# Delta-rule copies with a scale, and the causal mask, on other engines, under a planner that puts two engines' reads of one PSUM tile in sequence

## The chip, the cores and the metric

The kernel runs on one core of a Trainium2 chip. A core has five engines with instruction streams of their own: TensorE (PE in the profile; its weight loads are listed as PEld), VectorE (DVE), ScalarE (ACT), GpSimd (POOL) and SyncE (SP), which here issues the DMAs. TensorE writes its results to PSUM, in eight banks; DVE and ACT read them there. The engines wait for one another through semaphores.

The metric is the device time of one execution in microseconds. The time before is the median of three runs.

## The reference

One inference step of a decoder trunk of two layers, in float32, for 512 prompt tokens and 8 x 8 sample tokens that share all weights; the model width is 1024. Layer 0 mixes by pooling, layer 1 by a gated delta rule; each mixer is followed by a SwiGLU feed-forward block (width 2816), and all of it sits between RMS norms. The change lies in the gated delta rule. In the reference it is, for each of 16 value heads, chunk by chunk:

```python
decay = jnp.exp(jnp.where(causal, gc[..., :, None] - gc[..., None, :], -jnp.inf))
kb = k * beta[..., None]
a_mat = jnp.where(strict, jnp.einsum('bhnid,bhnjd->bhnij', kb, k) * decay, 0.0)
...
qk = jnp.einsum('bhnid,bhnjd->bhnij', q, k) * decay
q_dec = q * jnp.exp(gc)[..., None]
k_dec = k * jnp.exp(gc[..., -1:] - gc)[..., None]
...
v_new = u_i - jnp.einsum('bhck,bhkv->bhcv', w_i, S)
o_i = jnp.einsum('bhck,bhkv->bhcv', qd_i, S) + jnp.einsum('bhcs,bhsv->bhcv', qk_i, v_new)
S = S * gl_i[..., None, None] + jnp.einsum('bhck,bhcv->bhkv', kd_i, v_new)
```

Here u and w are solutions of a unit lower triangular system with a_mat; q and k are normalised, with 8 heads of their own, each shared by two value heads.

## The kernel before

**How the order comes about.** The kernel's functions don't issue instructions; they record them in a list (Plan.put, line 334). At the end Plan.finish (line 400) simulates the core with a table of costs (Plan.cost, line 283), chooses the order in which each engine's instructions are issued (Plan.forward, line 537; an instruction recorded as EITHER goes to DVE or POOL as the plan decides), and emits them. That is why nearly all rows of the profile name line 447, where they are emitted. A long list of numbers (CHOSEN, line 79) stirs the ranks of the instructions in one stretch of planned time after another: each number gives one shift, written down beforehand, and the shifts are applied in turn (Plan.refined and Plan.moved, lines 449 and 468). Where the plan foresees a wait of TensorE it fills it with matmuls of ones (tile ps_w). Any change of a cost, of an operation or of a number in the list therefore changes the order of everything behind it, DMAs included.

In its simulation an instruction waits for its operands, for its engine and, on TensorE, for the free bank. Two engines that read one PSUM tile are free to overlap in it. The cost of issuing a DMA on SP is 400 or 350 ns by size (2500 between two DRAM tensors).

**Tiling.** Channels lie on the 128 partitions and tokens along the free axis. Prompt tokens are cut into four spans of 128; the 64 sample tokens ride along as a fifth. The big products use float32r matmuls in three passes (a high and a low part of weights and activations): each block of weights is loaded as wraw, ACT copies its high part into wh, and DVE or POOL subtracts to get wl (Weights.split). The small products of the delta rule are plain float32 matmuls.

**The delta-rule stage.** The 16 value heads are done in four groups G of four. project(G) (line 1425) makes q, k and v of a group: projection, a convolution of width four along time (tiles u and ac, three multiply-adds on DVE for each chunk), Silu, and transposes. Its finish (line 1463) gets the norms of q and k; there nk, rq, bet and gcq are scaled for the group. v of the prompt (vt) and of the samples (vs) is scaled out of PSUM by nk. core(G) (line 1789) then does the rule itself: QD gets the differences of the cumulated gates gc, loaded from DRAM (gc_d) by one DMA for each span, has the mask bar added (0 on and above the diagonal, -1e30 below it) and goes through Exp; products of q and k give Uw (the triangular matrices) and QD. inv32 (line 1318) inverts blocks of 32 by some sixty DVE operations (tiles ia and ii), braided with sample_front (line 1586); small matmuls build the whole inverse; then scan (line 1720) and sample_heads (line 1650) run side by side.

In scan, for each span s and each head pair hd: pk is the product of the state S with k and q; rs (DVE) subtracts the scaled first part from vt; t1 (DVE) is the second part scaled by gcq; pv is the inverse times rs; vn is pv scaled by bet (DVE), and ve is vn scaled by kde (EITHER); S grows by kt times ve; po is QD times vn, and vt gets po scaled by rq, plus t1. In the first span there is no state, so t1 and rs are left out and vt is po scaled by rq alone (DVE). The next span's pk waits for S, so ve lies on the chain from span to span, and t1 doesn't.

sample_heads does one step of the same kind for the 64 sample rows against eight loaded states (St), with rs on the lower and t1 on the upper 64 partitions of one pk bank; ve is split there into a high part vH (ACT) and a low part vL (EITHER) for float32r matmuls.

While core(G) waits on its chains, the plan has the projections of group G + 1, the gate's projections (zz) and the output of group G - 1 (zgate) to fill in. zgate scales vt, transposes it on TensorE and multiplies it by z, which is loaded from DRAM (vt from z_d).

Of the kernel before, what the change touches and what calls it, by code (L numbers as in the profile page):

```python
# [11 lines left out]
F32 = mybir.dt.float32  # L12
F32R = mybir.dt.float32r
I32 = mybir.dt.int32
AF = mybir.ActivationFunctionType
ALU = mybir.AluOpType
PSUM = bass.MemoryType.PSUM
DRAM = bass.MemoryType.DRAM
SB = bass.MemoryType.SB

P = 128
# [5 lines left out]
SMP = NB * NT  # L27
# [29 lines left out]
class Plan:  # L57
# [2064 lines left out]
```

## Time and profile before

| what | us |
|---|---|
| median of three runs | 1546.24 |
| lowest and highest of them | 1545.52 to 1547.1 |
| the profiled execution's own time | 1548.15 |
| its span, first to last instruction | 1546.4 |

The chain that ended last names PE for 85% of the span, DVE for 10%, DMAs for 2%. By stages the span is, roughly: pooling mixer up to 100 us, feed-forward of layer 0 up to 470, the delta rule up to about 1065, its output and the feed-forward of layer 1 to the end. The table of costs is the planner's own; every duration in this document is from the profile.

How to read what follows: a busy time is the union of an engine's instructions, so matmuls that overlap in the pipeline count once, and a wait that is shorter than the tail of the matmul before doesn't show as idle time. In groups of instructions, the columns are line, engine, operation, output <- inputs, shapes (partitions x elements), count, then the busy time in us, the mean ns of one, and the idle time ahead of them with what ended it. In tables by stretch of time, each row gives the stretch, its length and the busy us (and count) of PE, PEld, DVE, ACT and POOL, then the granted clock of TensorE, the DMA engines' share and GB/s.

### The profile page before, as it was taken

The page shows a single profiled execution, that of the slowest core. Times are in us where ns is not written, and L with a number is a line of the kernel's source. Part 1 is how long each engine was busy: PE and PEld are TensorE (multiplying, and loading weights), DVE is VectorE, ACT ScalarE, POOL GpSimd, SP SyncE. Part 2 cuts the span into 40 slices and gives each one's busy share as a digit, 9 for nine tenths or more (in the row PEclk, how much of TensorE's full clock was granted, in tenths as well). Part 3 has the DMA queues.
Part 4 walks back from the last instruction along what each step waited for, and adds up shares of the span by engine and source line. Part 5 has one row for each costly group of instructions (what it writes and reads, how often), then busy time and mean ns, then how long its engine had stood idle before and what let it go on. Part 6 is the DMA issues. An engine that isn't in the chain of part 4 may idle for free.

```text
span 1546.4 us, 30413 instructions
## 1 busy us (share of the span) xinstructions
PE 1522.8 (98%) x11899; PEld 1466.0 (95%) x11899; DVE 1181.3 (76%) x2360; ACT 791.1 (51%) x1655; POOL 130.4 (8%) x274
## 2 busy tenths in 40 slices
PE   8999999999999999999999999999999999999997
PEld 8999999999999998899899799899999999999997
DVE  5993566667787798997999799677896476757855
ACT  7753443435555965553553563525564543434553
POOL 4110000000000010221221210100110000000000
PEclk9999999999999999999999999999999999999999
DMA  6464333233466523345243343656855432323263
GB/s 187 127 194 116 90 87 92 88 89 109 135 177 173 147 82 109 93 122 141 72 139 106 108 141 113 198 156 208 246 172 159 120 94 85 99 79 110 77 172 107
DMA packets 344902, 197.86 MB, mean 128 GB/s; under 512 B 13547, under 2 KB 337740, under 8 KB 344751
## 3 DMA queue, kind: packets, MB, share of 16 engines
q1 hardware_dynamic: 344759, 195.92, 44.0%
q8 instruction: 94, 1.54, 0.4%
q14 instruction: 49, 0.40, 0.1%
HBM read 165.60 MB, written 30.52 MB: 127 GB/s over the span
## 4 chain that ended last, share of the span: by engine, by line
PE 85%; DVE 10%; DMA 2%; issue 1%; ACT 1%; POOL 0%; DVEq 0%; SPq 0%; ACTq 0%; POOLq 0%
PE ps_B L447 28%; PE ps_A L447 26%; PE ps_m L447 17%; PE ps_s L447 5%; PE ps_k L447 4%; PE ps_x L447 2%; PE ps_n L447 1%; PE ps_e L447 1%; DVE wl L447 1%; DVE Uw L447 1%; DVE ii L447 1%; DVE ac L447 1%; DMA vt<-z_d 1%; PE ps_g L447 1%; DMA QD<-gc_d 0%
## 5 line engine op out<-in xcount | busy, mean ns | idle before, releaser
L447 ACT ACTIVATE wh<-wraw 128x1024 fp32r<-128x1024 f32 (+4 forms) x240 | 233.4, 976 | 223.1 <-PE ps_A L447 79.5
L447 DVE TENSOR_TENSOR wl<-wraw,wh 128x1024 fp32r<-128x1024 f32 (+4 forms) x232 | 257.9, 1117 | 78.2 <-ACT wh L447 49.8
L447 PE MATMUL ps_m<-hH,wh 128*128 128x320 f32 (+1 forms) x832 | 249.5, 312 | 0.5 <-ACT u L447 0.3
L447 PE MATMUL ps_m<-hL,wh 128*128 128x320 f32 (+1 forms) x832 | 245.1, 306 | 0.3 <-DVE hL L447 0.3
L447 PE MATMUL ps_m<-hH,wl 128*128 128x320 f32 (+1 forms) x832 | 241.2, 305 | 0.0
L447 PEld LDWEIGHTS ps_m<-hH,wh 128*128 128x128 f32 x832 | 154.3, 189 | 5.6 <-issue 1.1
L447 PEld LDWEIGHTS ps_m<-hL,wh 128*128 128x128 f32 x832 | 154.5, 189 | 3.0 <-issue 0.6
L447 PEld LDWEIGHTS ps_m<-hH,wl 128*128 128x128 f32 x832 | 153.3, 189 | 2.0 <-issue 0.8
L447 PE MATMUL ps_B<-hH,wh 128*128 128x320 f32 (+1 forms) x444 | 128.3, 305 | 0.1
L447 PE MATMUL ps_B<-hH,wl 128*128 128x320 f32 (+1 forms) x444 | 127.9, 304 | 0.0
L447 PE MATMUL ps_B<-hL,wh 128*128 128x320 f32 (+1 forms) x444 | 127.5, 303 | 0.0
L447 PE MATMUL ps_A<-hL,wh 128*128 128x256 f32 (+1 forms) x432 | 120.4, 291 | 0.0
L447 PE MATMUL ps_A<-hH,wh 128*128 128x256 f32 (+1 forms) x432 | 119.7, 292 | 0.0
L447 PE MATMUL ps_A<-hH,wl 128*128 128x256 f32 (+1 forms) x432 | 119.1, 290 | 0.0
L447 PE MATMUL ps_B<-aH,wh 128*128 128x288 f32 x352 | 99.7, 298 | 0.2 <-DVE xa L447 0.2
L447 PE MATMUL ps_A<-aH,wl 128*128 128x288 f32 x352 | 99.3, 295 | 0.0
L447 PE MATMUL ps_A<-aH,wh 128*128 128x288 f32 x352 | 98.8, 297 | 0.2 <-DVE y L447 0.2
L447 PE MATMUL ps_B<-aL,wh 128*128 128x288 f32 x352 | 98.5, 297 | 0.0
L447 PE MATMUL ps_A<-aL,wh 128*128 128x288 f32 x352 | 97.9, 295 | 0.0
L447 PE MATMUL ps_B<-aH,wl 128*128 128x288 f32 x352 | 97.8, 296 | 0.0
L447 PEld LDWEIGHTS ps_B<-hH,wh 128*128 128x128 f32 x444 | 81.5, 188 | 1.3 <-ACT wh L447 0.5
L447 PEld LDWEIGHTS ps_B<-hH,wl 128*128 128x128 f32 x444 | 81.8, 188 | 0.1
(468 smaller groups left out, 4045.4 us busy)
## 6 DMA issues: line engine op xcount, KB each, us to landing
wraw<-in_ffn_w_in_dram SPq DMA_DIRECT2D x77, 512.0 KB
wraw<-in_gdn_w_in_dram SPq DMA_DIRECT2D x56, 512.0 KB
graw<-in_ffn_w_in_dram SPq DMA_DIRECT2D x33, 512.0 KB
wraw<-in_ffn_w_out_dram SPq DMA_DIRECT2D x32, 448.0 KB
wraw<-in_gdn_w_out_dram SPq DMA_DIRECT2D x24, 512.0 KB
wraw<-in_ffn_w_out_dram SPq DMA_DIRECT2D x32, 320.0 KB
St<-in_state_gdn_rec_dram SPq DMA_DIRECT2D x32, 256.0 KB
out_dram<-St SPq DMA_DIRECT2D x32, 256.0 KB
```

Of the source, the lines that this page charges most:

```text
L447: calls[e](*a, **k)
```

## The change

The planner:
- Plan.forward keeps, for each PSUM tile, when each engine's last read or write of it ends. An instruction on PE, ACT, DVE or POOL that touches a PSUM tile which another engine touched before is planned to end no earlier than if it had started behind that engine's end.
- An issue on SP is planned at 520 or 480 ns above 16384 elements (520 where the tile has two dimensions) and 460 or 360 below.
- The list of numbers is another one (four strings instead of five).

The operations:
- bk, a new small tile, is bet times kde, made once for each head pair (8 products of 128 x 10 in all).
- scan: t1 goes from one DVE product of 256 columns to two ACT copies of 128 columns with a scale for each partition; ve goes from EITHER, out of vn, to two ACT copies straight out of pv, with scale bk; vt of the first span goes from DVE to one ACT copy.
- sample_heads: t1 likewise; ve is no longer stored: vH is two ACT copies of pv scaled by bk, and vL two DVE operations, pv times bk minus vH.
- project: vs goes from DVE to ACT.
- core: the mask is no longer a tile that is added but an affine_select on POOL. The tile bar is gone.

```diff
@@ Plan.cost
-            hold = 2500.0 if out.space == DRAM and ins[0].space == DRAM else 400.0 if m > 16384 else 350.0
+            flat = len(list(out.ap)) == 2
+            hold = 2500.0 if out.space == DRAM and ins[0].space == DRAM else \
+                (520.0 if flat else 480.0) if m > 16384 else 460.0 if flat else 360.0
@@ Plan.forward
-            elif e in past:
-                if past[e][1] or ops[i][11]:
-                    late = max(past[e][0] + self.REBASE - t, 0.0)
-                    hold, done = hold + late, done + late
-                past[e] = t + done, ops[i][11]
+            elif e != "SP":
+                late = 0.0
+                for name in ops[i][10]:
+                    for other, end in read.get(name, {}).items():
+                        if other != e:
+                            late = max(late, end + self.LAT[e] - t)
+                if e in past and (past[e][1] or ops[i][11]):
+                    late = max(late, past[e][0] + self.REBASE - t)
+                hold, done = hold + late, done + late
+                if e in past:
+                    past[e] = t + done, ops[i][11]
+                for name in ops[i][10]:
+                    read[name] = {**read.get(name, {}), e: t + done}
@@ masks
-        bar = cst.tile([P, P], F32, name="bar")
-        DVE.tensor_scalar(bar, t_gt, -1e30, None, op0=mult)
@@ project, finish
+                            DVE.tensor_tensor(bk[:, :, h2], bet[:, :, h2], kde[:, :, h2], op=mult)
...
-                    DVE.tensor_scalar(vs[:SMP, i], pv, nk[:SMP, SPANS, kh:kh + 1], None, op0=mult)
+                    ACT.activation(vs[:SMP, i], pv, AF.Copy, scale=nk[:SMP, SPANS, kh:kh + 1])
@@ sample_heads
-                DVE.tensor_tensor(t1, pk[up, 0].rearrange("p (e v) -> p e v", e=2),
-                                  gcq[up, SPANS, h2].unsqueeze(2).to_broadcast([SMP, 2, P]), op=mult)
+                for e in range(2):
+                    ACT.activation(t1[:, e], pk[up, 0, e * P:(e + 1) * P], AF.Copy,
+                                   scale=gcq[up, SPANS, 2 * kh + e:2 * kh + e + 1])
...
-                EITHER.tensor_tensor(ve, vn, kde[:, SPANS, h2].unsqueeze(2).to_broadcast([P, 2, P]), op=mult)
...
-                split2(ve, vH, vL)
+                for e in range(2):
+                    by = bk[:, SPANS, 2 * kh + e:2 * kh + e + 1]
+                    ve = pv[:, 0, e * P:(e + 1) * P]
+                    ACT.activation(vH[:, e], ve, AF.Copy, scale=by)
+                    DVE.scalar_tensor_tensor(out=vL[:, e], in0=ve, scalar=by, in1=vH[:, e].bitcast(F32),
+                                             op0=mult, op1=sub)
@@ scan
-                        DVE.tensor_tensor(t1, pk[:, 1].rearrange("p (e v) -> p e v", e=2),
-                                          gcq[:, s, hh].unsqueeze(2).to_broadcast([P, 2, P]), op=mult)
+                        for e in range(2):
+                            ACT.activation(t1[:, e], pk[:, 1, e * P:(e + 1) * P], AF.Copy,
+                                           scale=gcq[:, s, hh.start + e:hh.start + e + 1])
...
-                    EITHER.tensor_tensor(ve, vn, kde[:, s, hh].unsqueeze(2).to_broadcast([P, 2, P]), op=mult)
+                    for e in range(2):
+                        ACT.activation(ve[:, e], pv[:, 0, e * P:(e + 1) * P], AF.Copy,
+                                       scale=bk[:, s, hh.start + e:hh.start + e + 1])
...
-                        DVE.tensor_scalar(vv, pov, rqc, None, op0=mult)
+                        ACT.activation(vv, pov, AF.Copy, scale=rqc)
@@ core
-                EITHER.tensor_tensor(de, de, bar.unsqueeze(1).to_broadcast([P, 4, P]), op=add)
+                POOL.affine_select(de, de, [[0, 4], [1, P]], ALU.is_ge, -1e30, base=0, channel_multiplier=-1)
```

More of the change, by code (lines that the diff above doesn't have):

```diff
@@ L557, in forward @@
             past = {"DVE": (0.0, False), "ACT": (0.0, False)}
+            read = {}
         else:
             todo, left, taken, free, ready, avail, when, mode, dma, port, phases, fast, recent, busy, turn, still, \
-                quiet, past = state
+                quiet, past, read = state
             left, taken, when, recent = left[:], taken[:], when[:], recent.copy()
-            free, mode, port, turn, still, quiet, past = (dict(v) for v in (free, mode, port, turn, still, quiet, past))
+            free, mode, port, turn, still, quiet, past, read = (
+                dict(v) for v in (free, mode, port, turn, still, quiet, past, read))
             ready = {e: v[:] for e, v in ready.items()}
@@ L704, in forward @@
         return (todo, left, taken, free, ready, avail, when, mode, dma, port, phases, fast, recent, busy, turn, still,
-                quiet, past, order, times)
+                quiet, past, read, order, times)
     def take(self, e, q, taken, mode):
@@ L798, in hybrid_kernel @@
     kde = sp.tile([P, SP1, VH], F32, name="kde")
+    bk = sp.tile([P, SP1, VH], F32, name="bk")
     gls = sp.tile([P, NB, VH], F32, name="gls")
@@ L859, in masks @@
         DVE.scalar_tensor_tensor(out=eye2, in0=eyo, scalar=par, in1=eye2, op0=mult, op1=add)
-        return t_gt, bar, s_le2, s_gt2, s_gt_r, s_in, s_st, eye2
+        return t_gt, s_le2, s_gt2, s_gt_r, s_in, s_st, eye2
     def dup(ap):
@@ L1308, in finish0 @@
                 pre_norm(tp, back[0], acc2, hf, G_MPRE + NC)
-            t_gt, bar, s_le2, s_gt2, s_gt_r, s_in, s_st, eye2 = masks(tp)
+            t_gt, s_le2, s_gt2, s_gt_r, s_in, s_st, eye2 = masks(tp)
             s_le = s_le2[:, :SMP]
@@ L1677, in sample_heads @@
                 sn = cp_.tile([P, 4, 2, P], F32, name="sn", tag="sn", bufs=1)
-                rs, t1, vn, ve = sn[lo, 0], sn[up, 1], sn[:, 2], sn[:, 3]
+                rs, t1, vn = sn[lo, 0], sn[up, 1], sn[:, 2]
                 for e in range(2):
```

225 rows, old and new, of the table CHOSEN are left out of this document.

## The prediction

> **What bounds the kernel now.** I read the page first: busy time by engine and the slices.
>
> ```profile
> PE 1522.8 (98%) x11899; PEld 1466.0 (95%) x11899; DVE 1181.3 (76%) x2360; ACT 791.1 (51%) x1655; POOL 130.4 (8%) x274
> ...
> DVE  5993566667787798997999799677896476757855
> ```
>
> TensorE (PE) is the bound of the whole: 1522.8 of 1546.4 us. The change takes no matmul away, so it can only win time in which PE stands still. VectorE (DVE) is at 76% in the mean, but its slices show mostly nines from the fifteenth to the twenty-fifth (541 to 966 us); that is the delta-rule core. So I split the span by stage.
>
> ```profile
> core 0: us, PE busy (x) PEld busy (x) DVE busy (x) ACT busy (x) POOL busy (x), PEclk, DMA share, GB/s
> 0.00:40.00 40.00, 35.43 (x230) 32.13 (x230) 24.02 (x67) 29.35 (x70) 16.39 (x75) 0.91 0.66 181
> 40.00:560.00 520.00, 519.14 (x3845) 509.82 (x3845) 383.14 (x692) 284.12 (x511) 25.28 (x40) 0.99 0.43 124
> 560.00:1040.00 480.00, 471.37 (x4101) 433.38 (x4101) 422.18 (x1010) 229.88 (x655) 79.70 (x150) 1.00 0.43 123
> 1040.00:1500.00 460.00, 459.89 (x3455) 456.02 (x3453) 327.34 (x551) 227.16 (x382) 9.00 (x10) 1.00 0.46 134
> 1500.00:1547.00 47.00, 36.92 (x280) 34.66 (x278) 24.60 (x43) 20.54 (x40) 0.00 (x0) 0.95 0.36 109
> ```
>
> In the two long stages around the core PE is idle for 0.86 and 0.11 us: nothing to win there, whatever the order of the work. Start and end hold 4.6 and 10.1 us, but none of the rewritten operations. The core, 560 to 1040 us, holds 480 - 471.37 = 8.6 us of idle PE beside a DVE that is busy 422.2 of 480 us (88%), while ScalarE (ACT) is at 229.9 (48%) and GpSimd (POOL) at 79.7 (17%). The planner also fills foreseen waits with dummy matmuls (tile ps_w), which count as busy; the same windows for that tile:
>
> ```profile
> 560.00:1040.00 480.00, 4.47 (x30) 4.04 (x30) 1.00 0.43 123
> ```
>
> Together 8.6 + 4.5 = 13.1 us of visible standstill in the core: the stock from which this change can draw. Shorter waits, which the modelled end of the matmul before covers, are not in it. Two rows of PE's waits and a few pieces of the chain that ended last tell what is late:
>
> ```profile
> PE ps_x L447 <- DVE vt L447: 3.1, 3, 2.2
> PE ps_k L447 <- DVE QD L447: 0.9, 2, 0.7
> ```
>
> ```profile
> 851.34 5.46 DMA vt<-z_d
> ...
> 874.09 0.42 ACT vH L447
> 874.52 0.07 issue
> 874.59 0.81 POOL vL L447
> 875.40 1.24 POOL ve L447
> ```
>
> DVE results end the largest waits, though behind the first (vt) stands a load of z_d that takes 5.46 us and that no edit touches. At 875 us PE waits for a product ve that stood 1.24 us on POOL: that operation is rewritten.
>
> **The change part by part.** What leaves DVE, by groups:
>
> ```profile
> L447 DVE TENSOR_TENSOR QD<-QD,bar 128x512 f32<-128x512 f32 x16 | 11.0, 685 | 1.5 <-DMA QD<-gc_d 1.5
> ...
> L447 DVE TENSOR_TENSOR t<-ps_k,gcq 128x256 f32<-128x256 f32 x24 | 10.0, 418 | 1.2 <-PE ps_k L447 1.2
> ...
> L447 DVE TENSOR_TENSOR ve<-vn,kde 128x256 f32<-128x256 f32 x20 | 8.3, 420 | 0.2
> ...
> L447 DVE TENSOR_SCALAR vs<-ps_x,nk 64x128 f32<-64x128 f32 x16 | 5.4, 338 | 0.3
> ...
> L447 DVE TENSOR_SCALAR vt<-ps_s,rq 128x256 f32<-128x256 f32 x8 | 3.8, 479 | 1.3 <-PE ps_s L447 1.3
> ...
> L447 DVE TENSOR_TENSOR sn<-ps_k,gcq 64x256 f32<-64x256 f32 x8 | 3.4, 427 | 0.3
> ...
> L447 DVE TENSOR_TENSOR sn<-sn,kde 128x256 f32<-128x256 f32 x6 | 2.5, 417 | 0.0
> ```
>
> The sum is 11.0 + 10.0 + 8.3 + 5.4 + 3.8 + 3.4 + 2.5 = 44.4 us. What DVE gets back: vL, now 16 products of 128 columns straight from PSUM instead of the 5 that DVE had, and bk, 8 small products.
>
> ```profile
> L447 DVE SCALAR_TENSOR_TENSOR rs<-ps_k,ngc,vt 128x128 f32<-128x128 f32 x48 | 15.2, 345 | 2.1 <-PE ps_k L447 1.9
> ...
> L447 DVE TENSOR_TENSOR vL<-sn,vH 128x256 fp32r<-128x256 f32 x5 | 2.1, 417 | 0.0
> ```
>
> ```profile
> 966.13 0.24 DVE L447 TENSOR_TENSOR gcq<-gce,rq 128x10 f32<-128x10 f32 x2
> ```
>
> vL: 16 x 0.345 - 2.1 = +3.4; bk: 8 x 0.12 = +1.0. Net DVE: -40.0 us, 9% of its work in the core. The single bar product (one 128x128 operation, under the 0.35 us of such a shape) is outside it.
>
> ACT takes the copies with a scale per partition. The trace has no PSUM copy of 128 columns with a scale, so the nearest rows:
>
> ```profile
> L447 ACT ACTIVATE zz<-ps_m 128x256 f32<-128x256 f32 x16 | 6.0, 376 | 4.0 <-PE ps_m L447 4.0
> ...
> L447 ACT ACTIVATE y<-ps_A,prm 128x256 f32<-128x256 f32 x8 | 3.6, 472 | 2.6 <-PE ps_A L447 2.6
> ...
> L447 ACT ACTIVATE S<-ps_s 128x128 f32<-128x128 f32 x16 | 3.5, 274 | 8.1 <-PE ps_s L447 8.0
> ...
> L447 ACT ACTIVATE vH<-sn 128x256 fp32r<-128x256 f32 x8 | 3.3, 414 | 14.0 <-DVE sn L447 9.5 <-POOL sn L447 4.6
> ```
>
> A scale tile adds 472 - 376 = 96 ns at 256 columns; on S's 274 that makes 370 ns (ends: 274 if it adds nothing, 472 if the width doesn't matter; I take 370, nearest to S's shape). 48 (t1 in the scan) + 64 (ve) + 16 (vs) + 16 (t1 of the samples) + 16 (vH) = 160 copies x 0.37 = 59.2, plus 8 x 0.472 for vt, less the 3.3 of the old vH: +59.7 us (44 to 76 by the ends). ACT in the core goes from 230 to at most 290 of 480 us, 60%. ACT also splits the weights for the projections (wh) and empties their banks; what is queued behind a new copy there is late by 0.4 to 0.7 us, and the slack of an ACT that is idle half the time hides it. I cost it at nothing; if the cover fails, the second rival has the price.
>
> POOL loses its share of ve, ve of the samples and vL, and gets 16 affine_selects:
>
> ```profile
> L447 POOL TENSOR_TENSOR ve<-vn,kde 128x256 f32<-128x256 f32 x12 | 8.6, 722 | 13.4 <-DVE vn L447 10.4 <-DVE rv L447 3.0
> ...
> L447 POOL TENSOR_TENSOR vL<-sn,vH 128x256 fp32r<-128x256 f32 x3 | 2.3, 759 | 4.3 <-ACT vH L447 4.3
> ...
> L447 POOL TENSOR_TENSOR sn<-sn,kde 128x256 f32<-128x256 f32 x2 | 2.1, 1067 | 3.3 <-DVE sn L447 3.3
> ...
> L447 POOL TENSOR_SCALAR_AFFINE_SELECT eyo<-eyo 128x512 f32<-128x512 f32 x1 | 1.2, 1162 | 0.1
> ...
> L447 POOL TENSOR_SCALAR_AFFINE_SELECT eye<-eye 128x512 f32<-128x512 f32 x1 | 0.8, 833 | 0.0
> ```
>
> -13.0 us against 16 x 0.83 to 1.16 = +13.3 to 18.6: POOL stays near 80 of 480. On its path a mask takes 0.15 to 0.48 us more than DVE's 0.685, but it no longer queues on the busiest helper. The 16 loads from gc_d stay on SP; new there are only the planner's numbers for an issue. Every queue gets a new order; since the two long stages have no idle PE, I put that at zero, with 2 us either way for start and end.
>
> The new wait: two readers of one PSUM tile on two engines come one after the other. Before has such a pair, on one bank of ps_k:
>
> ```profile
> 570.99 0.41 DVE L447 TENSOR_TENSOR sn<-ps_k,ident 128x256 f32<-128x256 f32 x1
> ```
>
> ```profile
> 571.45 0.37 ACT L447 ACTIVATE sn<-ps_k 128x256 f32<-128x256 f32 x1
> ```
>
> ACT starts 0.05 us after DVE's end. In the scan this now holds for rs (DVE) with t1 (ACT), and for vn (DVE) with ve (ACT). Per step, pv to ve: before 0.42 + 0.05 + 0.42, or with POOL 0.72 to 1.24 at the end; after 0.74 if ACT goes first, or 0.42 + 0.05 + 0.74 = 1.21 behind vn. So between -0.97 and +0.32 us a step. With 12 of the 32 products leaving POOL I take zero.
>
> **The sum.** DVE relief of 40.0 us reaches the waits that end on DVE or POOL, not those on z_d: I let it take half of the 13.1 us, 6.5, and 1.5 more of the short waits that PE's busy time hides, 8.0 in all (ends: nothing; 13.1 + 5). The profiled execution took 1548.15 us, span 1546.4 and 1.75 around it; it becomes 1540.15. The median of the runs, 1546.24, lies 1.9 lower: 1538.2.
>
> How much the hidden part could be: the weight loads (PEld) fill 456.0 of 460 us after the core, 433.4 of 480 inside; at the same share, 0.991, the core's 433.4 us would pass in 437, 43 us less. That is no bound I can use, since the core's small matmuls load shorter weights. The Trainium skill, Trainium Kernel Development and Optimization, Performance Expectations, calls matmul busy time a bad metric and the LDWEIGHTS share a good one; by that rule the stock would be up to those 43 us rather than 13.1; the two rows fit it, but no row here separates short loads from standstill.
>
> **The rivals.**
> *More goes.* Short waits that no gap shows shrink too, as DVE's queue does: 16 us, 1530. For it: the weight-load share; against: many are the cost of changing between kinds of matmul, which stays.
> *A new chain, slower.* In the scan ACT's two copies of t1 go ahead of rs: 2 x 0.37 + 0.05 = 0.79 us on 3 steps of 4 groups, 9.5 us; ve lies behind vn, 0.32 x 16 = 5.1 us. 14.6 - 8.0 = +6.6: 1553. It decides once the order costs over 0.5 us on each of the 16 steps (8.0 / 16) and PE has no projection left to fill with. Against: ACT idle half the time, and the planner knows the order.
> *The waits stay.* PE stands for z_d (5.46 us at 851) and the start and end, and DVE's relief only lengthens its idle time: 0 to 3 us, 1545. The same comes out if the new order does not do what the planner's numbers say.
> *POOL holds DVE.* Beside eyo's affine_select a DVE product took far longer than its twin:
>
> ```profile
> 80.55 0.96 DVE L447 TENSOR_TENSOR aL<-nsq,aH 128x256 fp32r<-128x256 f32 x1
> ...
> 81.51 0.41 DVE L447 TENSOR_TENSOR aL<-nsq,aH 128x256 fp32r<-128x256 f32 x1
> ```
>
> 0.55 us held; 16 times that is 8.8 us of DVE back (18.6 if a whole select is held each time), so 31.2 instead of 40.0 go, and 6.2 of the 8.0 us: 1540. The Trainium skill, SBUF — State Buffer, section "SBUF: two separate sides", has the port that GpSimd shares with VectorE as an exclusive lock, against which a VectorE operation with two SBUF inputs waits in full; these two rows agree with it.
>
> **How the numbers follow.** Forecast 0.50 (1538, within 1533 to 1543); more goes 0.08; POOL holds DVE 0.12; the waits stay 0.17; slower 0.13. About 0.2% (3.1 us) is what a measurement of this kernel can tell from no change: faster is under 1543.1, 0.50 + 0.08 + 0.12 = 0.70; same 0.17; slower 0.13. The range runs to half of "more goes" and nearly to the slower case, 1530 to 1550, leaving out about 0.15.
>
> **What would show it.** Right: DVE in the core down by some 40 us, ACT up by some 60, ACT copies of 128 columns near 370 ns; idle plus ps_w in the core near 6 us; the stages around it unchanged; no PE wait for POOL ve. Wrong: idle plus ps_w still near 13, DVE's products beside the selects at 0.96, or a chain of waits in which ACT's t1 and ve alternate with DVE's rs and vn.

## The result and the profile after

| kernel | runs | median us | lowest to highest |
|---|---|---|---|
| before | 17 | 1546.44 | 1544.1 to 1551.24 |
| after | 17 | 1540.55 | 1531.94 to 1546.52 |
| before, later session | 11 | 1548.52 | 1547.04 to 1550.87 |
| after, later session | 6 | 1538.17 | 1536.1 to 1546.04 |

The ratio of after to before is 0.9949, 95% interval 0.9933 to 0.9964; in the later session 0.9944 (0.9924 to 0.9964). The forecast was 1538, range 1530 to 1550. The range takes in the time before as well, so meeting it says little; the sharper part of the forecast is 1533 to 1543. Note the spread: after scatters over 14.6 us, before over 7.1. The profiled execution of after took 1546.52 us (span 1544.5): it is the slowest of its 17, so its trace has to be read with its clock in mind (the share of its full clock that TensorE was granted; here 0.986 in the mean).

From the page of after, the busy times and three of the rows of slices:

```profile
PE 1519.8 (98%) x11879; PEld 1465.1 (95%) x11879; DVE 1160.7 (75%) x2288; ACT 831.8 (54%) x1811; POOL 122.7 (8%) x265
...
DVE  6794476658688698998899799557895576767854
...
PEclk9799999999999999999999999999999999999998
```

DVE is down by 20.6 us, ACT up by 40.7, POOL down by 7.7. The slices of DVE in the core still show mostly nines. The second slice of the granted clock, a 7, is new; before had a 9 there. The windows by stage of after:

```profile
0.00:40.00 40.00, 34.65 (x236) 31.98 (x237) 26.17 (x69) 29.90 (x73) 18.15 (x78) 0.91 0.69 181
40.00:560.00 520.00, 516.99 (x3789) 506.38 (x3788) 375.72 (x684) 273.19 (x497) 27.58 (x41) 0.98 0.43 122
560.00:1040.00 480.00, 474.10 (x4157) 438.02 (x4156) 408.61 (x951) 280.87 (x815) 65.34 (x138) 1.00 0.44 125
1040.00:1500.00 460.00, 458.93 (x3463) 455.94 (x3464) 329.22 (x551) 230.96 (x395) 11.64 (x10) 1.00 0.47 135
1500.00:1547.00 47.00, 35.11 (x242) 32.78 (x239) 20.99 (x38) 16.84 (x33) 0.00 (x0) 0.82 0.31 97
```

The same windows for the fillers, of after:

```profile
560.00:1040.00 480.00, 1.22 (x8) 1.08 (x8) 1.00 0.44 125
```

In the window that the prediction used, idle and fillers are 5.9 + 1.2 = 7.1 us, 13.1 before: down 6.0, and 56 more matmul records fall into the same 480 us. To follow the work and not the clock on the wall, cut the core at its own marks, from the first matmul into ps_m to the last into ps_x. Before, that is one window, with the row of the fillers behind it:

```profile
492.80:1069.20 576.40, 567.74 (x4788) 524.42 (x4786) 499.00 (x1174) 308.20 (x843) 88.76 (x167) 1.00 0.44 126
```

```profile
492.80:1069.20 576.40, 4.96 (x32) 4.34 (x32) 1.00 0.44 126
```

After, cut and filtered in the same way:

```profile
498.40:1064.70 566.30, 559.61 (x4760) 517.58 (x4758) 475.85 (x1106) 351.11 (x1001) 71.95 (x154) 1.00 0.46 128
```

```profile
498.40:1064.70 566.30, 2.53 (x16) 2.13 (x16) 1.00 0.46 128
```

The core is 10.1 us shorter: idle PE 8.66 to 6.69 (-2.0), fillers 4.96 to 2.53 (-2.4), and PE's busy time without fillers 562.78 to 557.08 (-5.7). The clock is 1.00 in both rows, so the last part isn't the clock. But the two windows don't hold quite the same matmuls: without fillers there are 4788 - 32 = 4756 before and 4760 - 16 = 4744 after. By tile, before has 10 more of ps_A and 5 more of ps_g and 3 fewer of ps_e, which is work at the edges of the core. At the mean of the row of after, 559.61 / 4760 = 0.12 us each, that is an estimated 1.4 us. The other 4.3 us I read as standstill that doesn't show as idle, since the modelled end of the matmul before covers it, and the gain of the core as some 8.7 us.

What the idle part consists of can be looked up. PE's wait for vt was 3.1 us before, and two of its three pieces, 0.73 and 2.23 us, stand behind a load of z_d. After, one such piece is left, of 1.65 us. These are the two products that end the longest piece, before and then after:

```profile
856.89 0.75 DVE L447 SCALAR_TENSOR_TENSOR vt<-ps_x,prm,vt 128x512 f32<-128x512 f32 x1 [5.33 <-DMA vt<-z_d]
```

```profile
854.36 0.75 DVE L436 SCALAR_TENSOR_TENSOR vt<-ps_x,prm,vt 128x512 f32<-128x512 f32 x1 [5.46 <-DMA vt<-z_d]
```

So 1.3 of the 2.0 us of idle time come from the waits that the prediction had put out of reach of a lighter VectorE, since VectorE itself stands for the load there.

But the core begins at 498.4 instead of 492.8, 5.6 us late, and from its end to PE's last instruction after takes 3.3 us more (473.0 for 469.7), so that only 1.9 of the 10.1 us are left in the two spans. Where they went shows in a stretch of the pooling mixer, here of before and then of after:

```profile
45.40:62.30 16.90, 16.90 (x107) 16.04 (x108) 13.99 (x39) 11.03 (x28) 1.46 (x2) 0.80 0.53 156
```

```profile
42.00:45.30 3.30, 2.76 (x18) 2.11 (x16) 3.30 (x11) 2.87 (x9) 0.00 (x0) 1.00 0.00 0
45.40:62.30 16.90, 16.90 (x67) 15.54 (x68) 10.24 (x27) 8.45 (x23) 2.48 (x3) 0.50 0.32 97
62.40:70.00 7.60, 7.60 (x66) 7.44 (x65) 6.22 (x20) 4.52 (x7) 0.00 (x0) 1.00 0.69 197
```

PE is busy all of the 16.9 us in both, but after gets a clock of 0.50 throughout and finishes 67 matmuls instead of 107. Near the end, 1502.9 to 1509.5 us, after runs at 0.50 once more, and before doesn't. A shorter stretch of half clock, 472.0 to 475.4 us, lies just ahead of the core of after.

```profile
1502.90:1509.50 6.60, 6.22 (x31) 6.06 (x32) 4.91 (x9) 2.86 (x6) 0.00 (x0) 0.50 0.30 86
```

The clock also orders the runs. Over the 17 runs of after the mean granted clock goes from 0.986 (1546.52 us) to 0.996 (1531.94 us); the correlation is -0.90 and the slope 13.9 us for 0.01. So most of the spread of after goes with the clock. Its median clock is 0.992, where before's later runs (34) have theirs at 0.994. The line isn't a law of the chip: over those 34 runs of before the slope is only 5.1 us for 0.01 and the correlation -0.47.

### The profile page after: what moved, and what is told of

It is laid out like the page before. It is cut to its first block, busy times and chain, and to the rows that moved or that the text cites. A ratio compares the mean times of both kernels' runs of the same rounds, so it can differ in the third digit from the quotient of the medians.

```text
span 1544.5 us, 30415 instructions
## 1 busy us (share of the span) xinstructions
PE 1519.8 (98%) x11879; PEld 1465.1 (95%) x11879; DVE 1160.7 (75%) x2288; ACT 831.8 (54%) x1811; POOL 122.7 (8%) x265
## 4 chain that ended last, share of the span: by engine, by line
PE 84%; DVE 10%; ACT 2%; DMA 2%; issue 1%; SPq 0%; DVEq 0%; ACTq 0%
PE ps_B L436 29%; PE ps_A L436 26%; PE ps_m L436 15%; PE ps_s L436 5%; PE ps_k L436 4%; PE ps_x L436 2%; PE ps_n L436 2%; DVE ia L436 2%; DVE wl L436 1%; PE ps_e L436 1%; DVE ii L436 1%; DVE ac L436 1%; DVE Uw L436 1%; PE ps_g L436 0%; DVE nacc L436 0%
## 5 line engine op out<-in xcount | busy, mean ns | idle before, releaser
L436 PE MATMUL ps_m<-hH,wh 128*128 128x320 f32 (+1 forms) x832 | 246.4, 309 | 0.2 <-ACT u L436 0.2
L436 DVE SCALAR_TENSOR_TENSOR ac<-u,cwt,ac 128x600 f32<-128x600 f32 x96 | 80.4, 847 | 2.1 <-ACT ac L436 2.0
```

What stands on the lines that cost most here:

```text
L436: calls[e](*a, **k)
```

## The experiments

Most of the following kernels keep one order frozen and exchange what is emitted at a planned place. The hook is this, with one lambda for each exchanged operation:

```diff
@@ Plan.finish
                 calls, _, a, k = ops[i][:4]
+                if i in self.alt:
+                    self.alt[i]()
+                    continue
                 calls[e](*a, **k)
```

All times are medians, and before ran beside each group of kernels: 1548.52, 1548.44 and 1548.29 us.

### The change again

No edit.

> The changed kernel again, untouched, on the chip on which the next runs go. Theory C (the gain lies in the core, 560 to 1040 us, because VectorE is lighter there; the stages around it give some back): 1540 us at a granted clock near 0.991, ratio 0.995, and over its runs the time falls with the granted clock, about 14 us for each 0.01. Theory O (the gain is the new order alone) expects the same of this run. If the spread of its runs has nothing to do with the clock, the slope is absent and a fast run has the same clock as a slow one.

1538.17 us, ratio 0.9944 (0.9924 to 0.9964). Its six runs go from clock 0.987 (1546.04) to 0.995 (1536.1), and a line through them has 14.7 us for 0.01. So the gain repeats, and so does its tie to the clock. Its profiled execution (1546.04) repeats the core too:

```profile
498.30:1064.40 566.10, 559.82 (x4760) 517.55 (x4758) 475.52 (x1106) 351.49 (x1001) 72.78 (x154) 1.00 0.45 128
```

Its fillers are again 2.53 us. This is the core with which the following sections compare theirs. Both profiled executions of after are the slowest of their group; there is no trace of a fast one. A line through all 23 runs of after gives 1538.4 us at 0.992 and 1535.5 at 0.994: by that estimate, at before's clock after would be 11 to 13 us faster, which is near the 9 to 10 us that the core lost.

### The new order with the old operations

```diff
@@ scan, order of after kept
+                        plan.swap(lambda: nc.vector.tensor_tensor(t1, pk[:, 1] ..., gcq ..., op=mult))
@@ core, order of after kept
+                plan.swap(lambda: nc.vector.tensor_tensor(de, de, bar ..., op=add))
```

and so on for ve (pv times bk, on VectorE), vs, vt and the t1 of the samples.

> The order of the changed kernel, with the scaled copies t, t1, ve, vs, vt and the mask put back on VectorE, each in its planned place; only the splits vH and vL of the sample keep the new form. Theory C: VectorE has some 45 us more in the core, idle and filler of TensorE there go from 7.1 us back to 13 us or more, 1546 to 1552 us in all, no faster than the kernel before. Theory O: the order carries the gain, so 1539 to 1542 us and idle and filler in the core stay under 9 us. If the mask on GpSimd or the copies on ScalarE hold VectorE up (theory P), this is faster than the changed kernel: under 1539 us.

1564.72 us, ratio 1.0109 (1.009 to 1.0127): 26.5 us above after and 16 above before, more than any of the theories had. Its core, cut at the same marks:

```profile
497.90:1091.10 593.20, 570.98 (x4760) 521.62 (x4758) 507.59 (x1210) 307.05 (x849) 61.62 (x138) 0.99 0.43 123
```

27 us longer than after's; idle PE is 22.2 us, and PE's busy time without fillers is up by 11. Of these 11, up to 5 can be the clock: 10.2 us of this core ran at 0.50 (672.9 to 676.3 and 932.3 to 939.2 us), and by estimate a stretch at clock 0.50 costs at most half its length. The longest waits of PE in its core say what it waits for:

```profile
PE ps_k L444 <- DVE QD L444: 5.7, 4, 3.0
PE ps_s L444 <- DVE sn L444: 2.6, 5, 0.9
PE ps_x L444 <- DVE vt L444: 2.0, 2, 1.7
PE ps_s L444 <- DVE vn L444: 1.9, 4, 0.9
```

All four end on DVE. Theory O, that the order carries the gain, falls: this order is no order for the old operations. The test is a little harsher than its name, since all 32 products ve are on VectorE here, 12 of which GpSimd did in before; VectorE is busy for 507.59 us in this core, 499.00 in before's.

### The old order with the new operations

```diff
@@ scan, order of before kept
+                    plan.swap(three)   # make bk, vn on VectorE, then two copies ve on ScalarE from pv
                     EITHER.tensor_tensor(ve, vn, kde[:, s, hh] ..., op=mult)
+                    plan.swap(lambda: None)
```

and likewise for t1, vs, vt, the mask and the split of the samples.

> The order of the kernel before, with the copies on ScalarE, the mask on GpSimd and the splits of the sample in the new form; ve stands right behind vn, and bk is made at its first use. Theory C: lighter VectorE alone takes 3 to 7 us of the 13.1 us of idle and filler in the core: 1540 to 1543 us. Theory O: nothing, 1545 to 1548 us. Theory W (the new waits of ScalarE behind VectorE's rs and vn cost more than the shorter stream gains, unless the order is made for them): over 1548 us.

1553.81 us, ratio 1.0038 (1.0025 to 1.0052): slower than before by 5.3 us, as theory W said; theory C, by which the lighter VectorE alone wins 3 to 7 us, fails. VectorE is at 471.37 us in the core, lighter even than in after, and it helps nothing:

```profile
489.00:1074.80 585.80, 571.12 (x4788) 525.43 (x4786) 471.37 (x1095) 352.90 (x1004) 87.75 (x166) 0.99 0.44 124
```

The core is 9.4 us longer than before's: idle PE 14.7 us (+6.0), fillers 5.42, PE's busy time without them +2.9. The last can be the clock, with 6.8 us at 0.50 (858.7 to 862.1 and 875.8 to 879.2 us); the idle time isn't explained by it. What is late is in the groups of DVE and then of ACT:

```profile
L455 DVE SCALAR_TENSOR_TENSOR rs<-ps_k,ngc,vt 128x128 f32<-128x128 f32 x48 | 15.2, 344 | 8.6 <-ACT t L1788 5.0 <-PE ps_k L455 3.2
```

```profile
L1808 ACT ACTIVATE ve<-ps_s,bk 128x128 f32<-128x128 f32 x64 | 19.7, 367 | 21.9 <-DVE vn L1805 21.8
```

ACT waits 21.8 us for vn, which reads the same bank, before it may make ve; rs waits 5.0 us for ACT's t. TensorE feels it where it loads vL and ve as weights:

```profile
PEld ps_s L455 <- DVE vL L1728: 3.2, 5, 1.1
...
PEld ps_s L455 <- ACT ve L1808: 2.0, 4, 0.8
```

In after the weight loads wait 0.5 us for vL and 0.3 for ve. That fits the rival "a new chain, slower", with almost its time (1553): where the order wasn't made for the pairs of readers, they cost more than the lighter VectorE wins. These rows don't add up to the whole 6.0 us of idle time, and a part of it may be owed to any edit in a frozen order.

### Parts of the way back

Only t and ve of the scan on VectorE in after's order (24 products t and 32 ve, 56 in all and 23.3 us by their rows; the counts in the expectation are wrong):

```diff
@@ scan, order of after kept
+                            plan.swap(lambda: nc.vector.tensor_tensor(t1, pk[:, 1] ..., gcq ..., op=mult))
+                            plan.swap(lambda: nc.vector.tensor_tensor(ve, pv[:, 0] ..., bk ..., op=mult))
```

> The order of the changed kernel with only the copies t, t1 and ve put back on VectorE at their planned places (the form with all of them, the mask and vs, vt back took 1564.7 us, 26 us above the changed kernel). 80 halves leave ScalarE (64 ve, 16 t1 and 48 t are issued as pairs there) and VectorE gets 64 instructions of about 0.42 us, 27 us in all. If every microsecond that VectorE gets lies on the path of an order planned without it: 1553 to 1566 us. If the mask is what costs (16 times 0.67 us on VectorE, with the wait of QD for it): 1542 us or less.

1543.74 us, ratio 0.997 (0.9952 to 0.9988): 5.6 us above after's 1538.17, between the two times that were expected. In the profiles the core pays 11.1 us for the 23.3 given to VectorE (577.2 us against 566.1, with 3.4 us at half clock). Its runs had a median clock of 0.995, where after's line gives 1534.1; at equal clock the difference is nearer to 10. Only the mask on VectorE in after's order:

```diff
@@ core, order of after kept
+                plan.swap(lambda de=de: nc.vector.tensor_tensor(de, de, plan.bar ..., op=add))
```

> The order of the changed kernel with only the mask put back on VectorE (16 additions of bar, 684 ns each by the form with everything back, 10.9 us in all, while 16 selects of 635 ns leave GpSimd). With t, t1 and ve back the time was 1543.7 us, 5.5 above the changed kernel's 1538.2; with everything back 1564.7, 26.5 above. If the mask carries the rest: 1549 to 1558 us, since VectorE then waits in its own order for the transfer into QD and for nothing else that is new. If the parts only hurt together: 1538 to 1544 us.

1552.12 us, ratio 1.0021 (0.9998 to 1.0044): 14.0 us above after, as expected if the mask carries the rest, for 16 instructions that take 11.0 us. Part of that is the clock: the median of its ten runs is 0.988, where after's line gives 1544.0, so 8 at equal clock. Its core, 578.8 us, is 12.7 longer than after's and, other than after's, not wholly at full clock (13.7 us at 0.50, in three stretches):

```profile
490.50:1069.30 578.80, 564.44 (x4760) 521.74 (x4758) 483.07 (x1122) 352.15 (x1001) 61.29 (x138) 0.99 0.44 126
```

What is late is in the waits of PE there:

```profile
PE ps_k L444 <- DVE QD L444: 7.4, 4, 3.1
```

In after this wait was:

```profile
PE ps_x L436 <- DVE vt L436: 1.6, 1, 1.6
PE ps_k L436 <- DVE QD L436: 1.4, 3, 0.9
```

On GpSimd the mask runs beside VectorE once its load from gc_d has landed; on VectorE, in this order, it stands in line, and QD comes late. That is a matter of the order: in before the mask was on VectorE too, and PE waited 0.9 us for QD. The two parts give 14.0 + 5.6 = 19.6 of the 26.5 us of the whole; vs, vt, t1 of the samples and what the parts do together are in the other 6.9, which weren't taken apart. Which of the two is the larger can't be told: by medians the mask, at equal clock t and ve. The cores say the same as equal clock: with half of the half-clock time taken off, which is the most that it can have cost, t and ve cost 9.4 us and the mask 5.9 (the whole of them 22). A part of the lower clock may be the mask's own doing, through its waits.

### The start and the clock

Some matmuls of the start issued twice in after; nothing else. The expectation speaks of fourteen; the trace has 24 more than after (11903 for 11879):

```diff
@@ Plan.finish
+                if e == "PE":
+                    nth = self.nth = getattr(self, "nth", -1) + 1
+                    if 155 <= nth <= 213 and k.get("start") and self.size(a[0]) in (128, 256, 320):
+                        calls[e](*a, **{**k, "stop": True})
                 calls[e](*a, **k)
```

> The changed kernel with some fourteen matmuls between 34 and 62 us issued twice (the first of an accumulation each, so that the second overwrites the first): 2 to 3 us more of streaming in the stretch in which the granted clock is 0.5 for 17 us. Theory H (the half clock follows on windows of too little streaming, and it is what makes the start of the changed kernel longer): the half-clock stretch there is gone or under 7 us, first matmul into ps_m 3 to 6 us earlier, 1534 to 1538 us in all, granted clock 0.994. If the start is longer because of the order of its work and not the clock: 2 to 3 us later, 1542 to 1543 us, with the half-clock stretch as long as before or gone without a gain.

1540.68 us, ratio 0.994 (0.9928 to 0.9953). Its trace, in the windows shown above:

```profile
45.40:62.30 16.90, 16.90 (x134) 16.19 (x133) 14.05 (x44) 11.14 (x27) 2.50 (x3) 1.00 0.63 185
```

The half clock is gone from this window, twice the matmuls pass, and the first matmul into ps_m comes at 492.6 us instead of 498.3. Over its five runs the clock is 0.993 to 0.997 (after: 0.986 to 0.996). So the trace has what theory H expected of it, but the time isn't 1534 to 1538: this run's core is 5.9 us longer than after's, with a short stretch at half clock inside (at 725 us) and longer waits for vt behind z_d, here of this kernel:

```profile
PE ps_x L440 <- DVE vt L440: 3.7, 3, 1.9
```

What the clock gave, the doubled work and the core took back. The core's idle time is 4.1 us longer, 3.0 of it behind loads of z_d (4.3 us for 1.3 in the repeat of after), and the stretch at half clock, 3.4 us, can make up to 1.7 of the rest. It doesn't look like the chance of one execution: at 0.995, the median of its five runs, after's line gives 1534.1, and they took 6.6 us more. The order in the core is the same, and only its beginning differs (492.6 for 498.3 us); whether the loads of z_d lie worse for that wasn't tested. So cores of single traces compare within some 6 us only. That holds for the 10.1 us too, since before has one trace, and for the parts put back, whose cores begin at 488.8 and 490.5 us.

Whether the doubled matmuls drove the half clock away is another matter, for there is a witness without them. The kernels with the mask or with t and ve put back issue the same instructions as after on TensorE up to the core, and their profiles have:

```profile
45.40:62.30 16.90, 16.90 (x132) 16.08 (x131) 15.75 (x45) 12.33 (x28) 2.66 (x4) 1.00 0.63 187
```

(t and ve back), with the core beginning at 488.8 us, and 490.5 with the mask back. The same stream of matmuls reaches the core anywhere between 488.8 and 498.4 us, and from the core's end to PE's last instruction it takes 468.8 us (doubled matmuls) and 469.3 (everything back) to 473.0 (after). So the 5.6 and 3.3 us that the profile of after loses around the core come with the half clock of that run and not with the order of its work. That the order invites it is only hinted at by the medians (0.992 for 0.994), and that denser work keeps it off is not shown: the kernel with t and ve back has the same median clock, 0.995, without the doubled matmuls.

The Trainium skill, TensorE: Matmul & The Clock Gate, section "Part 1: The HAM clock gate", says that the array runs at half rate after an idle window of about 3.4 us, and that this window runs freely, so that where it falls differs from run to run. The halved clock and the difference between runs agree with these rows, and so does the length: the half clock comes in stretches of 3.41 us or whole multiples of it (17.07 and 3.41 us in after, 6.83 twice in before). An idle window isn't seen here, since PE's busy time is 2.76 of the 3.30 us ahead of the long stretch and 16.90 of 16.90 us within it, at clock 0.50. What the rows show in its place is a stream of small matmuls, 18 in the 3.3 us ahead of the half clock; since another run with the same stream was spared, no threshold can be read from them.

### The planner without the search

Four kernels with an empty list of numbers (CHOSEN), so that the order is the planner's first. With the rule on two readers, old or new operations:

```diff
-    CHOSEN = ( ... )
+    CHOSEN = ()
@@ Plan.forward, in the kernel without the rule
-                for name in ops[i][10]:
-                    for other, end in read.get(name, {}).items():
-                        if other != e:
-                            late = max(late, end + self.LAT[e] - t)
```

New operations, with the rule:

> The changed kernel with its planner, but with the list of chosen moves (CHOSEN) empty, so that the order is the planner's first one, without the search behind it. Theory S (the planner's rule on two engines that read one PSUM tile gives the order its fit to the new operations): within 10 us of the changed kernel, 1540 to 1550 us, and faster than the same without the rule. Theory L (the fit comes from the chosen moves, found by a search): 1555 us or more, and no different from the same without the rule.

New operations, without the rule:

> As the run before it (no chosen moves), and the planner's rule on two readers of one PSUM tile taken out as well, the operations those of the changed kernel. Theory S: 5 us or more above the run with the rule. Theory L: within 4 us of it, either way.

The kernel before:

> The kernel before, its own planner, with no chosen moves. Theory D (the moved operations are worth 5 us or more whenever the order is planned for them): at least 5 us above the changed kernel with its planner and no chosen moves. Theory L (what the change gains is the better outcome of a search): within 4 us of that run, either way, and both far above 1546 us.

Old operations (the functions of before) under the planner of after, with the rule and with its new prices for issuing DMAs:

> The operations of the kernel before with the changed planner (the rule on two readers of one PSUM tile, and its new prices for issuing transfers), no chosen moves. Fourth corner beside 1564.8 us (new operations, with the rule), 1585.3 (new operations, without) and 1586.6 (old operations, old planner). Theory S1 (the rule fits any of the operations): 1564 to 1572 us. Theory S2 (the rule pays only with the new operations, whose ScalarE copies read the tile that VectorE reads): 1580 to 1592 us.

And two with another seed for the planner's draws, first the change, then the kernel before:

```diff
-    ROUNDS, STIR, SEED = 40, (0.0, 0.0, 300.0, 1000.0, 3000.0), 2
+    ROUNDS, STIR, SEED = 40, (0.0, 0.0, 300.0, 1000.0, 3000.0), 3
```

> The changed kernel with its planner, no chosen moves, and the planner's random draws from another seed (3 for 2). If the 1564.8 us of the other seed stand for the planner: 1560 to 1570 us. If the planner's first orders scatter by as much as the steps above (theory N: 20 us between corners are the luck of one draw): 1575 us or more.

> The kernel before with its planner, no chosen moves, another seed (3 for 2). If the 1586.6 us of the other seed stand for that planner: 1581 to 1592 us, 15 us or more above the changed kernel with seed 3. Theory N: 1575 us or less, or within 8 us of the changed kernel with seed 3.

| first order, no chosen moves | seed 2 | seed 3 |
|---|---|---|
| new operations, rule (the change) | 1564.82 | 1591.45 |
| new operations, no rule | 1585.33 | |
| old operations, rule | 1581.64 | |
| old operations, no rule (before) | 1586.55 | 1590.42 |

With seed 2 alone this would have read as a clean result: only the rule and the new operations together win 20 us. The other seed ends that story: the change goes from 1564.8 to 1591.5 us by the draw alone, and with seed 3 it stands 1.0 us above before. First orders scatter by as much as the steps between the corners (theory N). Nor are the corners pure: all but the kernel before have the new prices of DMA issues as well, and these were never tried alone. A trace of the rule can be read, but no time: without it PE waits for ve, in the waits of the kernel without the rule

```profile
PE ps_s L329 <- ACT ve L329: 3.9, 11, 0.8
```

and in neither of the two kernels with it does a row of that kind appear; but VectorE's wait for t isn't shorter with it. It is 10.9 us without the rule, 9.4 with it, and with it and seed 3:

```profile
DVE rs L329 <- ACT t L329: 14.2, 14, 4.1
```

So the search behind the list is worth 26 to 53 us in after and 38 to 42 in before, several times the change. That the present list for the new operations came out 6 to 10 us better than the old one for the old operations can be the operations, the rule or a luckier search, and these runs can't tell. A new search for the old operations wasn't tried.

## Why the prediction was right, and where not

**The place and the number: right.** The gain is in the core (-10.1 us there, some 8.7 for equal matmuls); what moved around it in the profiles came with the clock.

**"VectorE's relief shortens PE's waits": not shown.** The time came out, but the rows don't tie it to this step. Most of the visible idle time that went, 1.3 of 2.0 us, stood behind loads of z_d, which the prediction had left out. The wait for QD rose from 0.9 to 1.4 us. And the kernel with the lightest VectorE in the core, the new operations in the old order (471.37 us), has 14.7 us of idle PE. Whether the operations, the rule or the search made the gain stays open.

**Half of the visible standstill, 6.5 us: right by the window used.** It was 6.0 between 560 and 1040 us, and 4.4 from mark to mark, in part by other waits than those meant.

**1.5 us of hidden standstill: too small.** PE's busy time without fillers fell by 5.7 us, of which some 4.3 are standstill. "More goes" had the direction right, not the 16 us. The 8.0 us of the sum are 8.7 to 10.1 by the trace; that the median still met the forecast (5.9 in one session, 10.4 in the other) is owed in part to what the clock took around the core, and that is luck.

**VectorE down by 40.0 us: right in durations, mis-sized in time.** What was listed did leave, but busy DVE in the core fell only from 499.00 to 475.85 us, 23.2. There are two reasons. Durations of single instructions overlap: all of DVE's add up to 1316.3 us before and 1285.3 after, 31.0 less, where the busy time fell 20.6. And the planner used the room to take work from GpSimd, for instance the products of vt and oss, 12 on VectorE and 4 on GpSimd before; after:

```profile
L436 DVE TENSOR_TENSOR vt<-vt,oss x15: 670/686/1123, 661.2 to 1055.2; 128x512 f32<-128x512 f32 x15
...
L436 POOL TENSOR_TENSOR vt<-vt,oss x1: 1050/1050/1050, 919.0 to 919.0; 128x512 f32<-128x512 f32 x1
```

**ACT up by 59.7 us: the same error, and one more.** The price was right, 368 ns for 370:

```profile
L436 ACT ACTIVATE ve<-ps_s,bk 128x128 f32<-128x128 f32 x64 | 21.4, 368 | 11.7 <-DVE vn L436 5.9 <-PE ps_s L436 5.2
L436 ACT ACTIVATE t<-ps_k,gcq 128x128 f32<-128x128 f32 x48 | 15.9, 366 | 7.9 <-DVE rs L436 3.8 <-PE ps_k L436 2.6 <-DVE vt L436 1.1
```

But 64 x 368 ns is 23.6 us, and the row says 21.4 busy; in the core ACT rose by 42.9 us. A queue gains the spacing of its instructions, not their durations. Besides, the new order needs four table loads fewer (29 before, 25 after), which the prediction didn't count; at 1283 ns each that is 5.1 us less for ACT. Here are 28 and 24 of them:

```profile
L447 ACT ACT_TABLE_LOAD x28 | 35.9, 1283 | 0.9 <-DVE QD L447 0.4
```

```profile
L436 ACT ACT_TABLE_LOAD x24 | 30.8, 1283 | 0.4
```

**The mask, 0.15 to 0.48 us longer on its path, cost at nothing: the reverse in after's order.** The selects took 0.63 us in the median, below both ends of the estimate (0.83 to 1.16), and in after's order the mask out of VectorE's queue is worth 8 us at equal clock and 14 by the medians. Against before it isn't shown to win anything, since PE's wait for QD was shorter there.

**"POOL holds DVE", 0.55 us for each select: the mechanism is there, at less than half the price.** From the timelines of POOL and then of DVE in after:

```profile
526.93 0.63 POOL L436 TENSOR_SCALAR_AFFINE_SELECT QD<-QD 128x512 f32<-128x512 f32 x1 [25.02 <-DMA QD<-gc_d]
528.22 0.63 POOL L436 TENSOR_SCALAR_AFFINE_SELECT QD<-QD 128x512 f32<-128x512 f32 x1 [0.66 <-DVE ac L436]
```

```profile
527.05 1.14 DVE L436 SCALAR_TENSOR_TENSOR ac<-u,cwt,ac 128x600 f32<-128x600 f32 x1 [0.75 <-ACT ac L436]
...
528.23 1.25 DVE L436 SCALAR_TENSOR_TENSOR ac<-u,cwt,ac 128x600 f32<-128x600 f32 x1
...
529.52 0.84 DVE L436 SCALAR_TENSOR_TENSOR ac<-u,cwt,ac 128x600 f32<-128x600 f32 x1
```

The product of 0.84 us takes 1.14 and 1.25 beside a select. Beside the 16 selects 12 instructions of VectorE are longer than their like, by 0.15 to 0.44 us, 3.7 us together, not 8.8. The estimate scaled wrongly from eyo's select, which took 1.16 us. The excess goes with what is left of the select when the product starts: 0.51 us left and 0.30 more, 0.62 and 0.41 in these two, and 0.72 and 0.55 beside eyo in before.

**The new wait of two readers at zero: right for this order only.** In after, rs waits 6.8 us for t and ve 5.9 us for vn, but PE waits for neither, and its weight loads wait 0.3 us for ve. In the order of before the same operations cost 5.3 us more than the old ones. The step should have said that the zero holds as long as the order is made for the pairs.

**The stages around at zero, 2 us for start and end: wrong for both profiled runs of after.** The first lost 5.6 us ahead of the core and 3.3 behind it, to stretches at half clock, and the repeat has the same stretches. The search for idle PE couldn't see them: PE is busy in them. The 2 us should have been some 7 either way, half the spread of after's runs, and with the clock as the reason and not the order.

## What to carry to other kernels

An operation that is moved and the order planned for it are one thing: here the new operations in the old order lost 5 us, the old operations in the new order lost 16, and only together they won 6 to 10. Where the order comes from random draws, judge an edit over several draws before you give it a number, since one draw moved this kernel by 27 us. Size what an engine gains or loses by the spacing of its instructions, look at which result it then delivers earlier, and set the granted clock beside every time: runs of one kernel moved by 14 us with it.

## What was not expected of the hardware

TensorE's granted clock fell to 0.50 for up to 17 us while the engine had matmuls in flight without a gap, in a stretch of small ones, and not in every run of the same stream; its stretches were whole multiples of 3.41 us, but for those that the end of the run cuts off. Neighbouring instructions on an engine overlap in the records: 2288 on VectorE add up to 1285.3 us in a busy time of 1160.7. Beside a GpSimd select of 0.63 us a VectorE instruction took 0.15 to 0.44 us longer, the more the earlier in the select it started.
